# Attention probabilities copied by transfer into a one-pass-type tile before they are turned, with turns, values and ends two steps later

## The chip, the cores and the metric

The kernel runs on one core of a Trainium2 chip. The core has a matrix engine (TensorE, PE in the profile; its weight loads are PEld), a vector engine (DVE), a scalar engine (ACT), a general engine (GpSimd, POOL) and a queue engine (SyncE, SP), which works only as an issuer of transfers here. Transfers move between the chip's memory (SBUF) and the device memory, or within SBUF, on sixteen DMA engines. The metric is device time in microseconds (us) from start to end of one launch, the median of three runs.

## The reference

Two token batches, 512 and 256 tokens of width 1024, go through the same two layers with shared weights. Each layer adds half a SwiGLU feed-forward, then a token mixer, then half a SwiGLU again, each behind an RMS norm. The mixer of layer 0 is a gated linear recurrence, that of layer 1 is windowed attention, the part that the change touches:

```python
q = rope_partial(q.reshape(B, T, Hq, d))        # 16 query heads of 64
k = rope_partial(k.reshape(B, T, Hk, d))        # 4 key heads, each for 4 query heads
s = einsum('bnqhgd,bnkhd->bnhgqk', qb, kband) * d ** -0.5     # a block of 128 queries, 3 blocks of keys
s = where(abs(kpos - qpos) <= 128, s, -inf)
m = maximum(max(s), sink)
p = exp(s - m)
denom = sum(p) + exp(sink - m)
o = einsum('bnhgqk,bnkhd->bnqhgd', p / denom, vband)
return o.reshape(B, T, Hq * d) @ w_o
```

All values are 32-bit floats.

## The kernel before, in words

**Types.** A product of full precision is made of three products of the one-pass type F32R, a 32-bit type: an operand is split into a high part (ACT, L319) and the rest (DVE, L320), and `mm3` (L314 to L316) multiplies high by high, high by rest and rest by high.

**Tiles.** The score, key, value and output tiles of the attention come from one pool, `big`, with 21 slots (SLOTS) of 6 KB a partition; a tile takes a slot from its first writing until its last reading. There are eight PSUM banks (`ps`) and eight temporary tiles `tA`.

**The attention pipeline.** `swa` makes 24 `Unit`s: for each of 4 key heads, the 4 blocks of 128 queries of the first batch and the 2 of the second. A unit holds 4 query heads. Its query block sees 2 blocks of keys at an end of its sequence and 3 in the middle (`nkb`), so 16 units have 2 and 8 have 3. `pipeline` gives each part of each unit a step and a rank and runs all parts in this order; unit i starts at step t = 4i:

- `query` splits the queries, `turn` transposes them on PE in the type F32R (L1365, through the helper at L1181);
- `scores` takes a `big` tile `sc`, makes the products of one head (L1376, L1377), and DVE adds the band, scales and finds the minimum of the negated scores (L1379);
- `exps` on ACT (L1392), `sink` and `denominator` (L1398 to L1405), and at the end of `denominator` POOL multiplies the four heads' probabilities in place by the inverse sum (L1408), one instruction a head;
- `probs(j)`, at step t + 7 + j, transposes the four heads' probabilities of key block j by four PE instructions with the 32-bit type (L1414) into one PSUM bank and splits the bank into a high and a rest tile;
- `values(j)`, at step t + 9 + j, multiplies both with the values (L1426, L1427), adding up over the key blocks in one bank;
- `finish`, at step t + 8 + nkb, copies the sums out (L1435) and puts the halves of heads in place: for units 0 to 20 (`moved`) by two transfers on SP (L1439) and two adding transfers on POOL (L1440, issued at L147), for the last three by ACT and DVE (L1442, L1445).

Between these parts stand `extra` pieces: pieces of the query projection (`proj_tok`, matmuls at L314 to L316) up to step 66, the splits of finished outputs (`split_out`) from step 50, and 24 pieces of the first half of the output projection (`out_proj`) from step 66 to step 100.5. Behind the pipeline come the last splits and the second half of the output projection.

**What sets the order.** The program text gives priorities. The library that builds the program places each engine's instructions ahead of time by a model of their durations and of when their operands are ready: a later instruction whose operands are ready can be put ahead of an earlier one that still waits. On the chip every engine then works through its own fixed list, and an instruction that waits holds those behind it. SP's list holds the weight loads (L160, L194), which wait until a raw weight tile has been read (RAWBUFS is 4), and the transfers of `finish`. POOL's list holds the multiplies L1408, the adding transfers of `finish`, which wait for SP's transfers to land, and weight sums by transfer.

Of the kernel before, what the change touches and what calls it, by code (L numbers as in the profile page):

```python
# [9 lines left out]
F32 = mybir.dt.float32  # L10
F32R = mybir.dt.float32r
# [5 lines left out]
P = 128  # L17
# [11 lines left out]
GQ = 4  # L29
# [23 lines left out]
class Trunk:  # L53
# [1259 lines left out]
    def pipeline(self, units, extra):  # L1313
        events = []

        def at(step, rank, *calls):
            events.append((step, rank, len(events), calls))

        for i, u in enumerate(units):
            t = 4 * i  # L1320
            u.moved = i < 21
            at(t - (3 if i else 5), 5, u.query)
            at(t - 2, 3.5, u.turn)
            for h in range(GQ):
                at(t + h // 2, 0, lambda u=u, h=h: u.scores(h))
            at(t + 2, 2, u.sink)
            for h in range(GQ):
                at(t + 1 + h // 2, 2, lambda u=u, h=h: u.exps(h))
            at(t + 2, 2, u.denominator)
            for j in range(u.nkb):  # L1330
                at(t + 7 + j, 1, lambda u=u, j=j: u.probs(j))
                at(t + 9 + j, 4, lambda u=u, j=j: u.values(j))
            at(t + 8 + u.nkb, 4, u.finish)
        for step, call in extra:
            at(step, 3, call)
        for _, _, _, calls in sorted(events, key=lambda e: e[:3]):
            for c in calls:
                c()


class Unit:
# [59 lines left out]
    def denominator(self):  # L1401
        nc = self.k.nc
        den, sk = self.den, self.sk
        nc.vector.tensor_add(den, den, sk)
        nc.vector.reciprocal(den, den)  # L1405
        for i in range(GQ):
            p = self.sc[:, i, : self.nk]
            nc.gpsimd.tensor_scalar(p, p, den[:, i : i + 1], 1.0, ALU.mult, ALU.mult)  # L1408

    def probs(self, j):  # L1410
        k = self.k
        pt = k.ps()
        for i in range(GQ):
            k.nc.tensor.transpose(pt[:, i * P : (i + 1) * P], self.sc[:, i, j * P : (j + 1) * P], k.ident)  # L1414
        hi, lo = k.tmp(512, F32R), k.tmp(512, F32R)
        k.split(pt, hi, lo)
        self.split[j] = (hi, lo)
# [142 lines left out]
```

## Time and profile before

| | |
|---|---|
| median of 3 runs | 2769.42 us (2768.85 to 2770.11) |
| span of the profiled execution, first to last instruction | 2767.2 us |
| busy: PE, DVE, ACT, POOL | 99%, 80%, 50%, 16% of the span |
| attention pipeline (2063 to 2240 us): PE busy | 174.83 of 177.00 us |
| turns of probabilities (L1414) | 224 instructions, 270/272/300 ns least, median, most |

For the profiled execution the span alone is given, no time of its own beside it; the 2.2 us between its span and the median of the runs stand for what lies before the first and behind the last instruction.

How to read it: a row of the timeline has the start, the length, the engine, the line, the operation, the tiles written and read, and how many instructions it merges; a wait stands in brackets with what ended it. Matmuls are pipelined, so the length of one (0.39 us for 512 columns) is longer than the spacing between two starts (0.23 us). A row of groups has the busy time, the mean length of one, and the idle time before it. Lines with a q behind the engine belong to its sequencer, which issues transfers and waits.

### The profile page before, as it was taken

To read this page: it belongs to the slowest core of one execution; us is meant where nothing else is said; L and a number is where in the kernel's file an instruction comes from. 1 tells how busy PE (TensorE), PEld (TensorE's weight loads), DVE (VectorE), ACT (ScalarE), POOL (GpSimd) and SP (SyncE) were. 2 spreads that over 40 slices of the span, in tenths; PEclk is the share of its full clock that TensorE was granted. 3 is DMA by queue.
4 is the path that set the end of the run, shared out by engine and by line. 5 is a ranking of instruction groups with operands and counts; after the bars stand their busy time and mean duration, and the time that the engine had idled before them with its cause. 6 is when DMAs were issued, how large, how long until landed. Compare 5 with 4: busy or idle time off the path is not lost.

```text
span 2767.2 us, 40933 instructions
## 1 busy us (share of the span) xinstructions
PE 2745.0 (99%) x15117; PEld 2554.8 (92%) x15117; DVE 2206.5 (80%) x3766; ACT 1386.0 (50%) x2589; POOL 453.0 (16%) x491
## 2 busy tenths in 40 slices
PE   8999999999999999999999999999999999999998
PEld 8999999989999889999999999999888889999998
DVE  8788788767887888788878887887847868788877
ACT  7344444634455675444445543444458855444443
POOL 2111121200000101211111121111105611211111
PEclk9999999999999999999999999999999999999999
DMA  6554554851122743655444355544424422655443
GB/s 172 130 125 114 126 140 124 227 161 39 39 62 66 205 119 78 143 134 131 115 117 121 78 145 134 126 119 118 130 73 111 89 69 73 145 134 130 114 118 107
DMA packets 352040, 325.22 MB, mean 118 GB/s; under 512 B 14216, under 2 KB 271200, under 8 KB 351840
## 3 DMA queue, kind: packets, MB, share of 16 engines
q1 hardware_dynamic: 303040, 224.56, 27.7%
q0 software_dynamic: 44496, 84.56, 17.4%
q10 hardware_dynamic: 4304, 13.49, 1.3%
q8 instruction: 118, 1.93, 0.3%
q14 instruction: 82, 0.67, 0.1%
HBM read 225.82 MB, written 15.73 MB: 87 GB/s over the span
## 4 chain that ended last, share of the span: by engine, by line
PE 96%; DVE 2%; ACT 1%; DMA 1%; issue 0%; DVEq 0%; POOL 0%; SPq 0%; ACTq 0%; POOLq 0%
PE ps L513 42%; PE ps L577 21%; PE ps L315 6%; PE ps L316 6%; PE ps L314 6%; PE ps L760 5%; PE ps L823 3%; PE ps L928 1%; PE ps L1414 1%; PE ps L904 1%; PE ps L385 1%; PE ps L1426 0%; PE ps L1376 0%; PE ps L1427 0%; PE ps L1377 0%; PE ps L1181 0%
## 5 line engine op out<-in xcount | busy, mean ns | idle before, releaser
L513 PE MATMUL ps<-big,w 128*128 128x384 f32 x6720 | 1169.3, 334 | 0.0
L513 PEld LDWEIGHTS ps<-big,w 128*128 128x128 f32 x6720 | 1165.9, 188 | 1.7 <-ACT tA L530 0.2
L208 ACT CAST w<-wr 128x512 fp32r<-128x512 f32 x600 | 415.8, 707 | 689.2 <-PE ps L513 274.9
L577 PE MATMUL ps<-w,big 128*128 128x512 f32 x2520 | 575.7, 390 | 0.0
L577 PEld LDWEIGHTS ps<-w,big 128*128 128x128 f32 x2520 | 472.7, 188 | 98.0 <-ACT big L319 0.4
L209 DVE TENSOR_TENSOR w<-wr,w 128x512 fp32r<-128x512 f32 (+1 forms) x520 | 438.0, 846 | 145.9 <-ACT w L208 123.9
L147 POOL DMA_DIRECT2D s<-wr x126 | 109.8, 878 | 1250.3 <-DMA s<-in_ffn_w_dram 432.0
L599 DVE SCALAR_TENSOR_TENSOR x<-ps,x 128x512 f32<-128x512 f32 x468 | 302.4, 686 | 10.1 <-PE ps L316 10.0
L314 PE MATMUL ps<-big,w 128*128 128x384 f32 x640 | 219.6, 345 | 1.2 <-ACT w L175 0.9
L315 PE MATMUL ps<-big,w 128*128 128x384 f32 x640 | 215.7, 337 | 0.7 <-DVE big L320 0.7
L316 PE MATMUL ps<-big,w 128*128 128x384 f32 x640 | 214.6, 335 | 0.0
L319 ACT CAST big<-tA 128x384 fp32r<-128x384 f32 x296 | 148.0, 513 | 115.4 <-DVE tA L545 37.0
L147 POOL DMA_DIRECT2D wr<-wr x109 | 94.9, 871 | 518.3 <-DMA wr<-in_ffn_w_dram 165.9
L760 PE MATMUL ps<-w,big 128*128 128x512 f32 x756 | 177.1, 392 | 0.1
L320 DVE TENSOR_TENSOR big<-tA,big 128x384 fp32r<-128x384 f32 x296 | 168.0, 578 | 6.7 <-ACT big L319 4.7
L209 POOL TENSOR_TENSOR w<-wr,w 128x512 fp32r<-128x512 f32 x80 | 137.4, 1718 | 197.8 <-ACT w L208 195.8
L760 PEld LDWEIGHTS ps<-w,big 128*128 128x128 f32 x756 | 140.6, 188 | 29.1 <-DVE w L320 0.6
L215 DVE TENSOR_TENSOR wr<-wr,wr 128x512 f32<-128x512 f32 (+1 forms) x120 | 123.3, 1027 | 25.9 <-issue 23.6
L314 PE MATMUL ps<-w,big 128*128 128x512 f32 x336 | 134.6, 401 | 0.1
L316 PE MATMUL ps<-w,big 128*128 128x512 f32 x336 | 131.8, 392 | 0.5 <-DVE big L400 0.5
L315 PE MATMUL ps<-w,big 128*128 128x512 f32 x336 | 131.8, 392 | 0.0
L315 PEld LDWEIGHTS ps<-big,w 128*128 128x128 f32 x640 | 120.6, 188 | 2.0 <-DVE big L320 1.7
(214 smaller groups left out, 3504.0 us busy)
## 6 DMA issues: line engine op xcount, KB each, us to landing
wr<-in_ffn_w_dram SPq DMA_DIRECT2D x264, 512.0 KB, 4.0
s<-wr POOLq DMA_DIRECT2D x126, 256.0 KB, 4.8
s<-in_ffn_w_dram SPq DMA_DIRECT2D x120, 256.0 KB, 3.2
wr<-wr POOLq DMA_DIRECT2D x80, 256.0 KB, 3.8
wr<-in_hg_w_in_dram SPq DMA_DIRECT2D x32, 512.0 KB, 3.9
wr<-wr POOLq DMA_DIRECT2D x29, 512.0 KB, 4.6
spill<-x ACTq DMA_DIRECT2D x12, 512.0 KB, 4.0
kept<-big POOLq DMA_DIRECT2D x8, 768.0 KB, 9.7
```

The costliest lines, as they stand in the source:

```text
L147: self.nc.gpsimd.dma_start(out, src, accum_op=ALU.add)
L208: nc.scalar.copy(h, src)
L209: (eng or nc.vector).tensor_sub(l, src, h.bitcast(F32))
L314: nc.tensor.matmul(out, a[0], b[0], start=first, stop=False)
L315: nc.tensor.matmul(out, a[0], b[1], start=False, stop=False)
L316: nc.tensor.matmul(out, a[1], b[0], start=False, stop=last)
L319: self.nc.scalar.copy(hi, src)
L320: self.nc.vector.tensor_sub(lo, src, hi.bitcast(F32))
L513: self.nc.tensor.matmul(ps, a[x], b[y], start=first and k == 0 and i == 0, stop=k == 3 and i == 2, skip_group_check=True,)
L577: nc.tensor.matmul(ps, a[x], w[y], start=name == chain and kp == 0 and q == 0, stop=kp == 1 and q == 2, skip_group_check=True,)
L599: self.nc.vector.scalar_tensor_tensor(x, ps, c, x, ALU.mult, ALU.add)
L760: nc.tensor.matmul(ps, x[:, sl], y, start=fresh and k == 0 and q == 0, stop=k == 3 and q == 2, skip_group_check=True,)
```

## The change

Turns, values and end of every unit stand two steps later in the pipeline's order. In `denominator`, after each second multiply, a transfer on SP's queue copies two heads' probabilities from the score tile into a new `big` tile `pr` of the type F32R (as plain 32-bit data, so nothing is converted): two transfers a unit. `probs` then reads `pr` and turns it by the helper `transpose_r` (L1181), which writes the PSUM bank as F32R with the F32R identity. The number of turns, of splits and of value products is the same.

```diff
             for j in range(u.nkb):
-                at(t + 7 + j, 1, lambda u=u, j=j: u.probs(j))
-                at(t + 9 + j, 4, lambda u=u, j=j: u.values(j))
-            at(t + 8 + u.nkb, 4, u.finish)
+                at(t + 9 + j, 1, lambda u=u, j=j: u.probs(j))
+                at(t + 11 + j, 4, lambda u=u, j=j: u.values(j))
+            at(t + 10 + u.nkb, 4, u.finish)
...
             nc.gpsimd.tensor_scalar(p, p, den[:, i : i + 1], 1.0, ALU.mult, ALU.mult)
+            if i % 2:
+                if i == 1:
+                    self.pr = self.k.big([P, GQ, 3 * P], F32R)
+                two = slice(i - 1, i + 1)
+                nc.sync.dma_start(self.pr[:, two, : self.nk].bitcast(F32), self.sc[:, two, : self.nk])
...
         for i in range(GQ):
-            k.nc.tensor.transpose(pt[:, i * P : (i + 1) * P], self.sc[:, i, j * P : (j + 1) * P], k.ident)
+            k.transpose_r(pt[:, i * P : (i + 1) * P], self.pr[:, i, j * P : (j + 1) * P])
```

## The prediction

> **What bounds the kernel now.** I read the page first, then the busy time by stretches, then TensorE's groups and waits in the attention pipeline, then single rows of its timeline, and last the queues of POOL and SP. The page's first and fourth parts say that TensorE (PE) is the bound, over the whole span and on the chain that ended last:
>
> ```profile
> PE 2745.0 (99%) x15117; PEld 2554.8 (92%) x15117; DVE 2206.5 (80%) x3766; ACT 1386.0 (50%) x2589; POOL 453.0 (16%) x491
> PE 96%; DVE 2%; ACT 1%; DMA 1%; issue 0%; DVEq 0%; POOL 0%; SPq 0%; ACTq 0%; POOLq 0%
> ```
>
> The change touches only the attention pipeline, from the first scores to about 2240 us. The next rows are its stretch (columns: window, length, busy us of PE, weight loads, DVE, ACT, POOL, then clock, DMA share, GB/s), the group of the turns that the change retypes, and the first and last score product:
>
> ```profile
> 2063.00:2240.00 177.00, 174.83 (x1003) 149.32 (x1002) 136.42 (x427) 140.10 (x380) 93.73 (x138) 1.00 0.40 86
> L1414 PE MATMUL ps<-ident_r,big 128*128 128x128 f32 x224 | 33.7, 273 | 0.4 <-ACT tA L319 0.4
> L1376 PE MATMUL ps<-big,tA x96: 274/286/424, 2064.2 to 2222.4; 128*128 128x256 f32 x64, 128*128 128x384 f32 x32
> ```
>
> PE is busy 174.8 of 177.0 us here, so only 2.2 us of idle time can be won back, and PE time that is saved shortens the kernel as long as no new wait eats it. The 224 turns are 56 calls of four. 93 steps lie between the first and the last score product (unit 23's last is at step 93): (2222.4 - 2064.2) / 93 = 1.70 us a step, so two steps are 3.4 us.
>
> **Part 1: the retyped turns (the gain).** How long four turns hold PE is read from starts: from the first turn to the start of the second matmul behind it, less the normal spacing of the first one. The rows are of PE's timeline (start, length, line, ... count): eight old turns, then four of the one-pass type, which the query side (L1181) has already:
>
> ```profile
> 2226.36 1.03 PE L1414 MATMUL ps<-ident_r,big 128*128 128x128 f32 x8
> 2227.15 0.48 PE L314 MATMUL ps<-w,big 128*128 128x512 f32 x1
> 2227.46 0.40 PE L315 MATMUL ps<-w,big 128*128 128x512 f32 x1
> 2227.69 0.39 PE L316 MATMUL ps<-w,big 128*128 128x512 f32 x1
> ...
> 2121.36 0.46 PE L1181 MATMUL ps<-ident_r,s 128*128 128x128 f32 x4
> 2121.65 0.47 PE L1426 MATMUL ps<-tA,big 128*128 128x512 f32 x1
> 2121.96 0.39 PE L1427 MATMUL ps<-tA,big 128*128 128x512 f32 x1
> 2122.19 0.60 PE L1414 MATMUL ps<-ident_r,big 128*128 128x128 f32 x4
> 2122.54 0.48 PE L314 MATMUL ps<-w,big 128*128 128x512 f32 x1
> 2122.86 0.40 PE L315 MATMUL ps<-w,big 128*128 128x512 f32 x1
> ```
>
> A 512-wide matmul spaces 2227.69 - 2227.46 = 0.23. Eight old turns: 2227.46 - 2226.36 - 0.23 = 0.87, so 0.435 for four; the lone four at 2122.19: 2122.86 - 2122.19 - 0.23 = 0.44. Four one-pass turns: 2121.96 - 2121.36 - 0.23 = 0.37. The difference is 0.065 to 0.07 from these rounded times; with the two-digit rounding its bounds are 0.05 and 0.09. I take 0.07: 56 x 0.07 = **-3.9 us**, bounds -2.8 and -5.0.
>
> A row also weighs on how large this can be at all: four old turns cost 0.44 us, 56 x 0.44 = 25 us for all of them, and one-pass turns still cost 0.37. The Trainium skill (FP8 and Floating Point Precision, "TensorE Precision Notes") says that true FP32 takes four passes through the array; if an old turn were four passes and the new one a single pass, three quarters would go, 18 us rather than 3.9. The rows here do not agree: 224 turns leave 224 records, and a turn of the one-pass type is only a sixth cheaper.
>
> **Part 2: the copies (the cost).** Each of 24 units gets two copies on SP's queue, 48 in all. A unit with two key blocks copies 2 x 256 KB (16 units), one with three 2 x 384 KB (8 units): 14.7 MB. These rows bound them (DMA issues: KB each and median us to landing; then a queue's packets, MB and share; then SP and POOL rows):
>
> ```profile
> big<-tA SPq DMA_DIRECT2D x42, 64.0 KB, 2.2
> s<-in_ffn_w_dram SPq DMA_DIRECT2D x120, 256.0 KB, 3.2
> wr<-in_ffn_w_dram SPq DMA_DIRECT2D x264, 512.0 KB, 4.0
> big<-kept SPq DMA_DIRECT2D x8, 768.0 KB, 8.6
> q1 hardware_dynamic: 303040, 224.56, 27.7%
> 2220.83 1.25 SPq L1439 DMA_DIRECT2D big<-tA  x2
> ```
>
> Issuing costs SP 0.6 us a copy (1.25 for two), 30 us in all on a queue that mostly waits. On the DMA engines 14.7 / 224.56 of the share of q1 is 14.7 / 224.56 x 27.7% x 2767 = 50 us of all sixteen, so the stretch's share rises from 0.40 to about 0.68: not full. The trace shows no copy of this kind within the chip's memory at this size, so its landing is bounded: 2.2 us (64 KB, the only plain copy between tiles) below and 8.6 (768 KB) above. I take 3.2 for 256 KB and 4.0 for 384 KB, by the rows nearest in size. POOL's four multiplies are unchanged; the copy of heads 0 and 1 goes after the second, so only the last copy's issue and landing stand behind POOL: 0.6 + 3.2 = 3.8 us, or 4.6.
>
> What covers it is the move of two steps (3.4 us) plus the room there is now between POOL's last multiply and the unit's first turn. The tightest unit (4), a tight one with three blocks (20) and the last (23), POOL first and then PE:
>
> ```profile
> 2100.43 2.59 POOL L1408 TENSOR_SCALAR big<-big,stat 128x256 f32<-128x256 f32 x4
> 2103.56 0.38 PE L1414 MATMUL ps<-ident_r,big 128*128 128x128 f32 x2
> ...
> 2205.54 3.67 POOL L1408 TENSOR_SCALAR big<-big,stat 128x384 f32<-128x384 f32 x4 [3.25 <-PE ps L1377]
> 2210.67 0.60 PE L1414 MATMUL ps<-ident_r,big 128*128 128x128 f32 x4
> ...
> 2225.93 1.83 POOL L1408 TENSOR_SCALAR big<-big,stat 128x256 f32<-128x256 f32 x4 [0.42 <-DVE stat L1405]
> 2231.90 0.60 PE L1414 MATMUL ps<-ident_r,big 128*128 128x128 f32 x4
> ```
>
> The room is 0.5, 1.5 and 4.1 us. With 3.4 more it is 3.9, 4.9 and 7.5, against 3.8, 4.6 and 3.8: covered, by 0.1 to 3.7. At the upper landing (8.6) units 4 and 20 would miss by some 5 and 4 us. What then queues behind the waiting turn on PE is all that PE has next, the following units' scores and the projection's pieces, and DVE's reductions wait for those. Each unit's turns now wait for two transfers instead of POOL's one count; such an extra wait of PE's loader has a row:
>
> ```profile
> L1414 PEldq EVENT_SEMAPHORE  x16: 51/51/51, 2070.9 to 2218.6; - x16
> ```
>
> 48 of them would be 48 x 0.051 = 2.4 us, mostly hidden, since the loader is busy 149 of 177 us and runs ahead. For small misses and these I put **+0.5 us**; bounds 0 and +10. Without the two steps the tight units would miss by 3 us each, so the delay is the copy's cover and no gain of its own.
>
> **Part 3: the later turns, values and ends.** No work is added, only order. At the front two calls' turns and values come later, and the query projection's pieces (L314 to L316) fill in; at the end the last unit's turns, values and sum come 3.4 us later and the output projection has to cover. It can: its pieces for the first four blocks don't read the last two units, and at 12 matmuls x 0.23 = 2.8 us a block there are 11 us of them in one half of the columns, more than 3.4. An end moves its two transfers on SP and two adding transfers on POOL (L147) along; they now queue behind copies of later units on SP, which wait for POOL, while POOL's adding transfers wait for SP's. That ring costs at most an issue each, 1.25 us, while POOL is busy 94 of 177 us. I take 0, bounds -2.2 (all idle time of today goes) and +4.
>
> The old score tile is free once copied, but the copy lives till the last turn: a unit holds tiles for about 13 steps rather than 9 or 10, so one more of the 21 slots. By the code some 18 to 20 are taken around steps 50 to 60 (8 of the layer input, 2 keys, 2 values, 1 band, 2 held queries, 2 sums, 1 to 3 outputs, with 2 units' scores on top). A short wait for a slot is possible there; 0, up to +5.
>
> **The sum.** -3.9 + 0.5 = -3.4 on a span of 2767.2: 2763.8. The median of the runs shown is 2769.4, 2.2 over that span; I keep the 2.2: **2766.0 us**. A measurement of this kernel can tell about 0.2% from no change, 5.5 us: 2763.9 to 2775.0 counts as the same.
>
> **The rivals.**
>
> *Old waits vanish too.* The idle 2.2 us and the slow restarts round it come when ACT is late:
>
> ```profile
> PE ps L1376 <- ACT tA L1367: 1.3, 2, 1.1
> 2168.47 0.62 PE L1414 MATMUL ps<-ident_r,big 128*128 128x128 f32 x4
> 2170.20 0.38 PE L1376 MATMUL ps<-big,tA 128*128 128x256 f32 x1 [1.10 <-ACT tA L1367]
> ```
>
> With two steps' more turns and values in reserve PE would have work there: -3.9 - 2.2 = -6.1, or 2763.3. Against it: ACT's own load at that place does not change, and list orders move such gaps rather than close them.
>
> *SP's queue becomes the wait (the slower side).* SP's rows start one after the other, and its weight loads wait until DVE has read a raw tile (waits row: us in total, times, longest):
>
> ```profile
> 2086.31 7.42 SPq L160 DMA_DIRECT2D wr<-in_sw_w_o_dram  x4
> ...
> 2197.39 1.24 SPq L1439 DMA_DIRECT2D big<-tA  x2
> 2203.95 0.37 SPq L160 DMA_DIRECT2D wr<-in_ffn_w_dram  x1
> ...
> 2236.03 2.70 SPq L160 DMA_DIRECT2D wr<-in_ffn_w_dram  x2
> SPq L160 <- DVE w L176: 22.0, 6, 13.9
> ```
>
> SP stands from 2198.6 to 2203.95 and from 2222.1 to 2236.03 before such a load. Were the copies of units 19 and 23 ordered behind these, unit 23's would land at 2236.4 + 0.6 + 3.2 = 2240.2, though its turns want it at 2231.9 + 3.4 = 2235.3: 4.9 us. Behind the load at 2203.95 a copy loses up to 5.3 and behind the four from 2086.31 up to 7.4, each less its spare room, by estimate 2 and 3 left: +10 in all, -3.9 + 10 = +6.1, 2775.5. It decides once SP is held longer than the spare room above, 0.1 to 3.7 us. For it: six such waits, 13.9 us the longest. Against: the program's order puts transfers that are ready ahead of a load that is not (2220.83 before 2236.03).
>
> *A slot is short.* Around 2150 a unit's scores wait for a slot, the query pieces are used up early, and PE stands later. The estimate is bounded by one unit's period, 4 x 1.70 = 6.8 us; I price 6: -3.9 + 6 = +2.1, 2771.5.
>
> *The turns don't get cheaper*, since both kinds load weights at the same pace: 0 + 0.5, 2769.9. The 0.37 of L1181 speaks against it.
>
> *Four passes become one*: if a new turn held PE a quarter as long as an old one, 56 x 0.75 x 0.44 = 18 us would go, 2751; the 0.37 all but rules it out. (It is the Trainium skill's rule named in part 1.)
>
> **How the numbers follow.** Forecast 0.42 (own range 2763 to 2768.5; its lowest 0.06 count as faster), old waits vanish 0.17 (0.15 faster), SP's queue 0.20 (0.16 slower), slot 0.13 (0.03 slower), no cheaper turns 0.05, four passes 0.03 (faster). Faster: 0.06 + 0.15 + 0.03 = 0.24; slower: 0.16 + 0.03 = 0.19; same 0.57. The range runs from 2761 (old waits with the upper bound of the turns, -5.0 - 2.2 - 1) to 2778 (SP's queue with a little over); left out are the four passes and the outer parts of the two rivals, 0.17.
>
> **What would show it.** Turns at L1414's place at 0.37 a call, 224 records; a wait of PE for a transfer into the new tile under 1 us; SP's copies issued within 1 us of POOL's multiply; idle PE in the stretch still near 2 us; and the matmuls behind the pipeline at their old pace. PE rows with a release by that transfer of several us, or a copy that starts right behind a load's long wait, would prove the forecast wrong upwards; an idle time near nothing, downwards.

## The result, and the profile after

The changed kernel takes 2787.33 us (median of four launches) against 2769.25 for the kernel before, measured beside it: a ratio of 1.0063 [1.0050, 1.0077], 18 us slower. The forecast was 2766.0 with 2761 to 2778 around it. The profiled execution spans 2785.3 us against 2767.2, the same 18. One of the four launches ran at a granted clock of 0.849 and took 3023.11 us; it is left out of the ratio and of every reading below.

The page's busy time and its chain of the work that ended last:

```profile
PE 2748.7 (99%) x15117; PEld 2552.8 (92%) x15117; DVE 2211.8 (79%) x3766; ACT 1385.0 (50%) x2589; POOL 449.0 (16%) x491
PE 92%; ACT 2%; DVE 2%; DMA 1%; POOL 1%; issue 1%; DVEq 0%; SPq 0%; ACTq 0%; POOLq 0%
```

The engines do the same work; on the chain PE holds 92% instead of 96, and ACT, POOL and waits without an owner take what it lost. Ahead of the attention pipeline PE's busy time agrees with the kernel before within 1 us in each of five stretches up to 2063 us, and behind the pipeline the matmuls keep their old pace. The pipeline's stretch, by the busy time of each engine (columns as in the prediction), is where the time went:

```profile
2063.00:2240.00 177.00, 163.11 (x923) 135.85 (x923) 131.04 (x406) 129.04 (x361) 87.57 (x132) 0.96 0.59 160
2120.00:2140.00 20.00, 14.47 (x78) 11.93 (x77) 10.67 (x32) 10.54 (x33) 8.10 (x13) 0.89 0.58 158
2180.00:2200.00 20.00, 17.58 (x91) 14.20 (x92) 17.46 (x53) 15.14 (x44) 9.40 (x16) 0.83 0.57 155
```

PE idles 13.9 of 177 us, where it was 2.2, and the stretch holds 923 matmuls instead of 1003. The granted clock, 1.00 for this stretch before, falls to 0.89 and 0.83 in the stretches with the stalls. The DMA engines' share rose from 0.40 to 0.59; the forecast had 0.68.

The waits of the same stretch, to 2260 us (us in total, times, longest), of the changed kernel:

```profile
PE ps L1181 <- DMA big<-big: 6.3, 6, 2.7
SPq L1413 <- POOL big L1408: 113.5, 43, 21.8
SPq L1444 <- ACT tA L319: 7.7, 7, 3.6
```

and of the kernel before:

```profile
SPq L1439 <- ACT tA L319: 94.4, 14, 34.5
```

SP used to stand at the ends' transfers (L1439), waiting for what ACT makes. Now it stands at the copies (L1413), waiting for POOL, 113.5 us in 43 waits, and the ends' transfers (now L1444) stand behind them. How that goes round is in single rows of the changed kernel's timeline, SP and ACT first, then POOL, then PE. The end here is that of unit 5, the copies are those of unit 7:

```profile
2116.66 0.60 ACT L1440 COPY tA<-ps 128x512 f32<-128x512 f32 x1
2122.95 1.59 SPq L1413 DMA_DIRECT2D big<-big  x2
2124.63 1.36 SPq L1444 DMA_DIRECT2D big<-tA  x2
...
2111.61 2.87 POOL L1408 TENSOR_SCALAR big<-big,stat 128x256 f32<-128x256 f32 x4
2121.43 2.58 POOL L1408 TENSOR_SCALAR big<-big,stat 128x384 f32<-128x384 f32 x4
2129.82 1.99 POOL L147 DMA_DIRECT2D big<-tA  x2 [5.81 <-DMA big<-tA]
2131.08 3.01 POOL L1408 TENSOR_SCALAR big<-big,stat 128x384 f32<-128x384 f32 x4
...
2126.01 0.34 PE L1181 MATMUL ps<-ident_r,big 128*128 128x128 f32 x2 [1.13 <-DMA big<-big]
2129.01 1.00 PE L1181 MATMUL ps<-ident_r,big 128*128 128x128 f32 x6 [2.66 <-DMA big<-big]
2130.36 0.63 PE L315 MATMUL ps<-w,big 128*128 128x512 f32 x1
2130.79 0.63 PE L316 MATMUL ps<-w,big 128*128 128x512 f32 x1
2132.45 0.39 PE L314 MATMUL ps<-w,big 128*128 128x512 f32 x1
2132.68 0.39 PE L1432 MATMUL ps<-tA,big 128*128 128x512 f32 x1
```

ACT had the sums of unit 5 ready at 2117.26, but SP issues their transfers at 2124.63, 7.4 us later, because the copies ahead wait for POOL's multiplies from 2121.43 on. Those transfers land, POOL's adding transfers start at 2129.82 after 5.81 us of waiting, and only behind them in POOL's list come the next unit's multiplies, at 2131.08, for which SP's next copies wait. On the way the ends' landing is slow: the two transfers issued at 2124.63, beside the copies, landed after 4.3 us (median), where 2.2 is the median of the kernel before. The multiplies follow each other at 2131.08 - 2121.43 = 9.65 and 2121.43 - 2111.61 = 9.82 us. A unit of two and of three key blocks alike has four steps, 4 x 1.70 = 6.8 us, so POOL loses some 3 us a unit for as long as the ring runs, until the reserve (probabilities multiplied and copied ahead of their turns) is used up and PE waits for copies: 1.13 and 2.66 us here. After the pause PE's matmuls start 2130.79 - 2130.36 = 0.43 us apart instead of 0.23 (2132.68 - 2132.45) for about 3 us more. The Trainium skill (TensorE: Matmul & The Clock Gate, "Part 1: The HAM clock gate") says that PE falls to half its clock after an idle window of about 3.4 us and returns after about as long a busy one; the trace agrees about the half and the time back. The two pauses here add up to 3.79 us, with two turns between them, so neither of them alone is as long as that window.

### The profile page after: what moved, and what is told of

Same layout as the page of the kernel before. It is cut to its first block, busy times and chain, and to the rows that moved or that the text cites. A ratio compares the mean times of both kernels' runs of the same rounds, so it can differ in the third digit from the quotient of the medians.

```text
span 2785.3 us, 41086 instructions
## 1 busy us (share of the span) xinstructions
PE 2748.7 (99%) x15117; PEld 2552.8 (92%) x15117; DVE 2211.8 (79%) x3766; ACT 1385.0 (50%) x2589; POOL 449.0 (16%) x491
## 4 chain that ended last, share of the span: by engine, by line
PE 92%; ACT 2%; DVE 2%; DMA 1%; POOL 1%; issue 1%; DVEq 0%; SPq 0%; ACTq 0%; POOLq 0%
PE ps L513 42%; PE ps L577 21%; PE ps L315 6%; PE ps L314 6%; PE ps L316 6%; PE ps L760 5%; PE ps L823 3%; PE ps L928 1%; DMA big<-tA 1%; PE ps L1181 1%; PE ps L904 1%; PE ps L385 1%; POOL big L1408 0%; ACT big L1392 0%; ACT w L175 0%
## 5 line engine op out<-in xcount | busy, mean ns | idle before, releaser
L147 POOL DMA_DIRECT2D s<-wr x126 | 110.4, 883 | 1252.5 <-DMA s<-in_ffn_w_dram 438.1
L319 ACT CAST big<-tA 128x384 fp32r<-128x384 f32 x296 | 148.0, 513 | 114.1 <-DVE tA L545 36.2
L147 POOL DMA_DIRECT2D wr<-wr x109 | 95.5, 876 | 516.4 <-DVE w L209 196.2
```

The costliest lines, as they stand in the source:

```text
L147: self.nc.gpsimd.dma_start(out, src, accum_op=ALU.add)
L319: self.nc.scalar.copy(hi, src)
```

## The experiments

All differences below are against the kernel before as it was measured beside each (2768.4 to 2769.3 us). The list of every engine is planned anew for each kernel, so each run also has small shifts that are not its edit's. The runs stand here by question, not in the order in which they were made, so an expectation may name the time of a run that stands further down.

The expectations set four theories against each other. *Ring*: SP's copies wait for POOL and hold the ends' transfers, for which POOL waits. *Landing*: the copies' own way takes too long for the turns. *Delay*: the two later steps are the loss. *Traffic*: the copies' bytes lengthen the ends' transfers, and others wait for these. An edit also moves the line numbers below it: the ends' transfers on SP are L1439, L1444, L1448 or L1453, the copies L1413, L1414 or L1422, POOL's adding transfers L147 or L148.

### The parts one by one

**The delay alone**: before, with the three steps changed as in the change, and nothing else.

> The kernel before with turns, values and ends two steps later, no copies, old turns. Ring theory (the copies wait for POOL's multiplies on SP's list and hold the ends' transfers behind them, POOL's adding transfers wait for those to land, and the next multiplies stand behind POOL's adding transfers): the delay alone does no harm, 2769 within 3 us, idle time of PE in the attention pipeline near the old 2.2 us. Rival 'delay' (two steps more of live tiles and the later end are the loss): 2780 or more. Rival 'landing' (the copies' own way through the loaded DMA engines is the loss): 2769.

Measured 2773.95 us, 1.0019 [1.0010, 1.0027]: +5.1. The waits of ACT, this run first and then the kernel before:

```profile
ACT big L319 <- DMA big<-tA: 6.0, 3, 3.3
```

```profile
ACT big L319 <- DMA big<-tA: 1.7, 1, 1.7
```

The splits of finished outputs (`split_out`, ACT at L319) kept their steps while the ends moved two steps towards them, so ACT now stands before ends that have not landed. The delay was priced at nothing; it is not, and the ring theory's 2769 within 3 us was missed by 2.

**The type alone**: before, with POOL writing its product into a new F32R tile, no copies and the old steps.

```diff
+        self.pr = self.k.big([P, GQ, 3 * P], F32R)
...
-            nc.gpsimd.tensor_scalar(p, p, den[:, i : i + 1], 1.0, ALU.mult, ALU.mult)
+            nc.gpsimd.tensor_scalar(self.pr[:, i, : self.nk], p, den[:, i : i + 1], 1.0, ALU.mult, ALU.mult)
...
```

The turns then read the new tile through `transpose_r`, as in the change. The writing rounds the probabilities to the one-pass type, so their rest parts are left out of the values; the instructions are the same in number.

> The kernel before at its old steps, without copies: POOL's multiply writes its product into a new tile of the one-pass type and the turns read that. POOL rounds the probabilities to that type, so their rest parts are left out of the result. This is the retyping alone: 56 calls of turns at 0.37 instead of 0.44 us, 2765 to 2766, if the gain of the turns is as worked out; 2769 if the retyped turns are no cheaper in place; above 2775 if one more live tile a unit is already too much for the 21 slots.

Measured 2769.19, 1.0000 [0.9991, 1.0009]: not the 2765 to 2766 of the turns' gain, and not above 2775, which would have shown that one more live tile is too much. The turns did get cheaper, by PE's rows of this kernel:

```profile
2229.44 0.45 PE L1181 MATMUL ps<-ident_r,big 128*128 128x128 f32 x4
2229.73 0.46 PE L314 MATMUL ps<-w,big 128*128 128x512 f32 x1
2230.03 0.40 PE L315 MATMUL ps<-w,big 128*128 128x512 f32 x1
```

and its stretch by busy time:

```profile
2063.00:2240.00 177.00, 173.20 (x1008) 146.15 (x1007) 137.66 (x430) 139.75 (x380) 93.86 (x138) 1.00 0.41 89
```

Four take 2230.03 - 2229.44 - 0.23 = 0.36, but PE is idle 3.8 us of the stretch (177.00 - 173.20) instead of 2.2, by waits in the planned order of this run. The profiled execution spans 2764.8, 2.4 less than that of before; the medians show nothing of it. PE time that is saved is not all won, even without copies.

**The bytes alone**: before, with 48 copies of the change's shapes out of the keys' tile into a tile that nobody reads.

```diff
+            if i % 2:
+                if i == 1:
+                    pr = self.k.big([P, GQ, 3 * P])
+                two = slice(i - 1, i + 1)
+                nc.sync.dma_start(pr[:, two, : self.nk], self.kT[:, :, : self.nk].bitcast(F32))
```

> The kernel before with its steps and its turns, and 48 copies of the same shapes from the keys' tile into a tile that nobody reads: the bytes and SP's issues alone, no wait on POOL, no delay. Traffic theory: 2774 to 2780, with the ends' SP transfers landing after 2.8 us or more (2.24 before, median). Ring theory: 2767 to 2771. Output unchanged, since nothing reads the copies.

Measured 2771.54, 1.0011 [1.0001, 1.0020]: +2.8, between what the two theories said.

**Delay and bytes**: both of these edits together.

> The kernel before with the two steps' delay and the 48 copies taken from the keys' tile, read by nobody: the order and the bytes of the change, with no transfer that waits for POOL and no turn that waits for a copy. The run with the change's own copies and old turns (2794.2) differs from this one only in that SP's copies wait for POOL. Ring theory: about the sum of delay (+5.1) and bytes (+2.8), 2775 to 2780, so that 14 us or more of the 2794.2 belong to SP's wait for POOL. If delay and bytes together make the loss without any wait of SP: 2786 to 2795.

Measured 2777.39, 1.0034 [1.0024, 1.0044]: +8.6, about the sum of 5.1 and 2.8, as the ring theory had it.

**Copies that nobody needs**: the changed kernel, but `probs` turns the score tile in the old type, as before.

```diff
-            k.transpose_r(pt[:, i * P : (i + 1) * P], self.pr[:, i, j * P : (j + 1) * P])
+            k.nc.tensor.transpose(pt[:, i * P : (i + 1) * P], self.sc[:, i, j * P : (j + 1) * P], k.ident)
```

> The changed kernel, but the turns read the score tile with the old type as before; the copies are made and nobody reads them. Ring theory: the queues are as in the changed kernel, POOL's multiplies still come every 10 us in the worst stretch; turns are spared only the copy's issue and landing of some 4 us and pay the old price (+4): 2778 to 2790. Rival 'landing': nobody waits for a copy, 2769 to 2772. Rival 'delay': 2780 or more, the same as the run with the delay alone.

Measured 2794.22, 1.0091 [1.0077, 1.0105], 4 us above the ring theory's range and far from *landing*. It differs from the run before it in the tile that the copies read, so that here SP's copies wait for POOL. Three views of each, a stretch by busy time, the group of the ends' adding transfers (busy, mean ns, idle before) and SP's waits, first with the copies that wait:

```profile
2110.00:2200.00 90.00, 78.11 (x399) 62.60 (x398) 58.60 (x184) 59.42 (x167) 44.65 (x66) 0.91 0.58 152
```

```profile
L147 POOL DMA_DIRECT2D big<-tA x42 | 41.7, 1132 | 66.5 <-DMA big<-tA 50.2 <-ACT tA L319 9.6 <-ACT big L319 3.5
```

```profile
SPq L1413 <- POOL big L1408: 126.1, 44, 21.8
```

then with the copies out of the keys' tile, where SP has no such wait:

```profile
2110.00:2200.00 90.00, 86.28 (x500) 72.66 (x499) 71.02 (x222) 71.58 (x205) 56.91 (x80) 1.00 0.69 176
```

```profile
L147 POOL DMA_DIRECT2D big<-tA x42 | 41.2, 1106 | 40.8 <-DMA big<-tA 12.1 <-ACT tA L319 7.9 <-ACT tA L1367 5.3
```

With the same bytes and the same steps, SP's wait for POOL, with the ends' transfers behind it, costs 2794.22 - 2777.39 = 16.8 us. POOL waits 50.2 us for ends' transfers instead of 12.1, PE does 399 matmuls in 90 us instead of 500, and the clock falls from 1.00 to 0.91. No turn waits for a copy here: the ring works through POOL's list alone. The Trainium skill (DMA: Bandwidth & Descriptors, "Anatomy of one DMA") says that a transfer's wait for a semaphore is done by the issuing sequencer, not by the DMA engines; the 126.1 us that SP stands, with ready transfers behind it, agree.

The way from before to after is then: delay +5.1, bytes +3.4 (2777.39 - 2773.95), SP's wait for POOL +16.8, and the new turns, which also wait for the copies, 2787.33 - 2794.22 = -6.9; in all 18.4, against the 18.1 measured. Of the -6.9 the turns' own time explains about 4; the rest was not settled.

### Longer delay

**Two steps more**: the changed kernel with turns, values and ends four steps later than before. If the copies' landing were the trouble, more time would hide it.

> The changed kernel with turns, values and ends four steps later than in the kernel before instead of two. Ring theory: the ring's 10 us a unit is a pace, which no later step can hide, 2785 to 2795. Rival 'landing': 3.4 us more cover the late copies, 2775 to 2780 with the longer end.

Measured 2811.26, 1.0155 [1.0140, 1.0170], 24 us worse than the change itself, and outside both ranges. No turn waits for a copy any more; PE's longest waits are for ACT's copies of the turned queries (L1367), and DVE's scores (L1379) wait for copies to land:

```profile
PE ps L1376 <- ACT tA L1367: 14.4, 3, 8.0
DVE big L1379 <- DMA big<-big: 12.3, 3, 8.0
```

So more time does hide the copies' landing from the turns, and the kernel is slower all the same: that they land too late for the turns is not the main cause. Part of the 24 us is another loss. By the code, a score instruction can wait for a copy only where its tile takes a slot that the copy still reads, and with two steps more every unit holds its tiles longer. At 2168.15 one such wait of 8.04 us ends; ACT's exponentials waited 9.67 us for the scores, and PE's wait of 7.96 us ends behind them.

### Cutting the ring

**No ends' transfers**: all ends by ACT and DVE (`u.moved = False`), in the kernel before and in the changed one.

> The kernel before with no unit's end moved by transfers: all ends go by ACT and DVE as the last three do. It is the partner of the next run, and costs DVE 21 x 0.85 us more: 2770 to 2785 by either theory.

> The changed kernel with all ends by ACT and DVE: copies stay on SP, but POOL has no adding transfers and SP no ends' transfers, so the ring does not exist. Ring theory: against its partner it is within +5 us (delay 5, turns -4, small misses) instead of the 18 us between the kernels before and after. Rival 'landing': 12 us or more over its partner.

Measured 2772.49, 1.0014 [1.0005, 1.0023], and 2775.58, 1.0025 [1.0016, 1.0035]. Without ends on the queues the whole change, copies, delay and all, costs 2775.58 - 2772.49 = 3.1 us instead of 18, within the 5 us that the ring theory gave. Nearly all of the loss goes through the ends' transfers. SP stands before the copies even longer here than in the changed kernel (113.5 us):

```profile
SPq L1413 <- POOL big L1408: 129.6, 47, 21.8
```

That SP stands costs little by itself; what stands behind it counts.

**Ends from ACT's queue**: `nc.scalar.dma_start(dst, r(low[:HD, :]))` in `finish`, in place of SP's.

> The changed kernel with one edit: the ends' two plain transfers go out on ACT's queue, right behind ACT's own copy out of PSUM, so that SP's list holds copies and weight loads only. Same copies, same bytes, same turns. Ring theory: the ends' transfers leave within 1 us of ACT's copy, POOL's multiplies come every 6.6 to 7 us again, and the time falls to 2764 to 2771 (the turns' gain of 4 less what 42 issues cost ACT). Rival 'landing': the copies move as many bytes, 2783 or more. Rival 'delay': 2783 or more.

Measured 2783.78, 1.0053 [1.0041, 1.0066]. The stall at 2120 is gone, by the busy time and PE's waits:

```profile
2120.00:2140.00 20.00, 19.99 (x123) 16.87 (x122) 15.03 (x53) 16.49 (x49) 12.57 (x18) 1.00 0.74 199
```

```profile
PE ps L1432 <- DVE tA L320: 4.8, 6, 1.6
PE ps L1376 <- ACT tA L1367: 4.5, 6, 1.5
```

but ACT now issues 42 transfers, and PE waits for what ACT and DVE make, 4.5 and 4.8 us, against 1.5 and 3.1 in the changed kernel. The ring is cut and most of its gain paid away; the ring theory's 2764 to 2771 was missed, and the time just reaches the 2783 of its rivals. What ACT's issues cost was not measured by itself.

**Adding transfers later**: POOL's adding transfers are kept back and issued behind the next unit's multiplies.

```diff
+        with self.k.tc.issue_after(last.ins):
+            while self.k.adds:
+                self.k.into(*self.k.adds.pop(0))
...
-                k.into(dst, r(low[HD:, :]))
+                k.adds.append((dst, r(low[HD:, :])))
```

> The changed kernel; POOL's two adding transfers of an end are put behind the next unit's four multiplies on POOL's list instead of ahead of them, so that no multiply stands behind a landing. Nothing else is moved; no engine gets more work. Ring theory: POOL waits some microseconds less for the ends' transfers, multiplies come every 6.8 us, PE waits for copies under 1 us in all, and the time is 2770 to 2776 (the delay's own 5 over the kernel before, less the turns' 4, plus small misses). Rival 'landing' (a copy's own 3 to 5 us through loaded DMA engines is the loss): 2782 or more.

Measured 2787.85, 1.0069 [1.0054, 1.0084]: as slow as the change and 12 us above the ring theory's range, with other rows, of the busy time, of the adding transfers' group, and of ACT's timeline:

```profile
2120.00:2140.00 20.00, 19.88 (x125) 17.08 (x125) 14.20 (x54) 15.56 (x48) 13.66 (x21) 1.00 0.81 216
```

```profile
L148 POOL DMA_DIRECT2D big<-tA x42 | 40.9, 1142 | 4.6 <-DMA big<-tA 4.0 <-issue 0.3
```

```profile
2174.59 0.40 ACT L320 CAST big<-big 128x256 fp32r<-128x256 f32 x1 [6.23 <-DMA big<-tA]
```

POOL waits 4.6 us in all before these transfers instead of 62.4, and PE runs through 2120 to 2140. But the outputs are finished a unit later, and ACT stands 6.23 us before a split of one (and 6.57 us once more near the end); right behind these two stand the copies and splits for which PE has its two longest waits of this run, 6.34 and 5.33 us.

**Copies behind the ends on SP**: a unit's copies are put on SP after the ends' transfers of the unit two before it; POOL's list stays.

```diff
+                while k.copies:
+                    k.copies.pop(0)()
```

(in `finish`, pinned behind its last transfer on SP; `denominator` only notes the copies, but for units 0, 1 and 23, which issue them at once.)

> The changed kernel, but the copies of a unit are put on SP behind the ends' transfers of the unit two before it, so that an end's transfer no longer stands behind a copy that waits for POOL; POOL's adding transfers stay in their place, unlike in the run that moved them. Ring theory: 2766 to 2774, ends' SP transfers within 1 us of ACT's copy, POOL's multiplies 6.5 us apart. Traffic theory: 2777 to 2785. If the copies now come too late for the turns, which would be a third thing, PE rows with a release by a transfer into the new tile add up to over 5 us.

Measured 2783.89, 1.0056 [1.0041, 1.0071]. The third thing of the expectation came, over its 5 us; the waits of PE and of SP:

```profile
PE ps L1182 <- DMA big<-big: 6.8, 9, 2.2
SPq L1453 <- ACT tA L320: 47.2, 9, 8.4
```

SP stands at the ends again, as before the change. PE's waits for copies stay, 6.8 us where the changed kernel has 6.3.

**Copies from POOL's own queue**: `nc.gpsimd.dma_start` for the copies.

> The changed kernel, but the 48 copies are issued from POOL's queue behind POOL's own multiplies, so that no SP instruction waits for POOL and the ring of SP and POOL has no SP half; the bytes are the same. POOL issues 48 more transfers of about 0.65 us, 31 us on an engine that was busy 94 of 177 us. If the ring is all that costs (ring theory): 2766 to 2773, POOL's multiplies some 6.5 us apart everywhere. If the copies' 14.7 MB lengthen the ends' 64 KB transfers, and the output's splits and the buffers of the ends wait for these (traffic theory): 2777 to 2785, with waits of ACT or DVE for the ends' transfers of 3 us and more.

Measured 2784.27, 1.0061 [1.0045, 1.0078], from 2781.47 to 2792.23, of which the profiled launch is the slowest. POOL, by its busy time in the stretch, has become the crowded list, 122.40 us instead of 87.57:

```profile
2063.00:2240.00 177.00, 163.37 (x904) 134.82 (x903) 126.20 (x396) 126.54 (x355) 122.40 (x174) 0.95 0.58 156
```

The ring theory's 2766 to 2773 and 2774 missed in both of these runs. The traffic theory's 2777 to 2785 holds in both by the time; its mechanism does not show in the first, where the ends' transfers on SP land after 2.1 us (median), and may in the second, where they take 3.1, against 2.2 in the kernel before and 2.8 in the changed one.

### The output's splits

If late splits were all that `adds_later` lost, moving the splits too should free it. They stand up to six steps later here, those of the second batch last:

```diff
-            extra.append(((50, 58, 83)[n // 4] + 2 * (n % 4), ...
+            extra.append(((50, 60, 85)[n // 4] + 2 * (n // 2 % 2) + (6 if n >= 4 else 4) * (n % 2), ...
```

**Both moves** on the changed kernel, **the splits alone** on it, **the splits with the delay alone**, and **both moves on the kernel before**:

> The changed kernel with two edits: POOL's adding transfers behind the next unit's multiplies (as in the run adds_later), and the splits of finished outputs of key heads 1 and 2 moved from steps 58 to 64 and 83 to 89 to steps 60 to 68 and 85 to 93, those of the second batch last, so that ACT does not stand before the adding transfers' landing. Two-cause theory (the ring on SP and POOL in the middle of the pipeline, and ACT standing at the splits after an end that comes later): both are gone, 2764 to 2770. If the copies' landing or the live tiles were the loss: 2780 or more.

> The changed kernel with the splits moved as above, and POOL's list as in the changed kernel. Two-cause theory: the ring stays, ACT's standing goes: 2778 to 2784. If the ring is no cause of its own: 2770 or less.

> The kernel before with turns, values and ends two steps later and the splits moved as above; no copies. Theory: the delay's loss of 5 was ACT standing 6 us at the splits: 2767 to 2771. If it is the later end of the pipeline instead: 2773 to 2775 as with the delay alone.

> The kernel before with the two edits of the run both, at the old steps and without copies: what these edits bring by themselves. By the theory nothing to gain but 1.7 us of ACT's standing: 2766 to 2770, so that a lower time of the run both would be the retyped turns'.

Measured 2783.73, 1.0056 [1.0041, 1.0071]; 2792.01, 1.0087 [1.0072, 1.0102]; 2771.43, 1.0012 [1.0003, 1.0022]; 2771.96, 1.0014 [1.0005, 1.0024]. The first two missed what the theory said, by 14 and 8 us; the first lies in the range named for the copies' landing or the live tiles, and why the second is slower than the change itself was not settled. The third comes 0.4 us above its range: the moved splits win back half of the delay's 5.1. The fourth comes 2 above: the moves cost some 3 us by themselves at the old steps. In the kernel with both moves one stall of PE is the largest, by rows of POOL, SP, DVE and PE:

```profile
2168.59 1.92 POOL L148 DMA_DIRECT2D big<-tA  x2
2169.23 1.12 SPq L161 DMA_DIRECT2D wr<-in_sw_w_o_dram  x2
2170.44 1.32 SPq L1448 DMA_DIRECT2D big<-tA  x2
2174.98 1.51 SPq L1414 DMA_DIRECT2D big<-big  x2
2178.90 0.69 DVE L321 TENSOR_TENSOR tA<-ps,tA 128x512 fp32r<-128x512 f32 x1 [5.08 <-DMA big<-tA]
2179.65 0.79 PE L1436 MATMUL ps<-tA,big 128*128 128x512 f32 x1 [4.67 <-DVE tA L321]
```

DVE writes a temporary tile there, of which there are eight, and it waits for ends' transfers that read such a tile: two issued on POOL from 2168.59 on, two on SP from 2170.44. The wait ends at 2178.90, 10.3 and 8.5 us after these two rows begin. By the rows of DMA issues the two on POOL landed after 6.1 and 9.5 us and the two on SP after 8.2 (median), where before the medians are 3.0 and 2.2. Beside them lie two weight loads of 512 KB at 2169.23 and copies.

**Both moves without copies, and with copies that nobody waits for**: turns of the old type, then the same with the 48 copies out of the keys' tile.

> The kernel with the adding transfers and the output's splits moved (2783.7), without the copies: turns read the score tile in the old type; the two steps' delay and both moves stay. If what remains of the loss there comes with the copies (their bytes): 2770 to 2775. If it comes with the order, that is the delay and the moves themselves: 2780 to 2784.

> The kernel with both moves and no copies (2777.2), plus the 48 copies from the keys' tile, read by nobody. If the bytes are what the uncut kernel (2783.7) still loses there: 2782 to 2787. If it is that turns and SP wait for POOL and for the copies: 2777 to 2780, the bytes' price of before.

Measured 2777.17, 1.0029 [1.0018, 1.0041], between the two ranges named for it, and 2784.30, 1.0054 [1.0039, 1.0069], in the range named for the bytes. The ends' transfers in the rows of DMA issues (KB each, median us to landing), without and then with those copies:

```profile
big<-tA SPq DMA_DIRECT2D x42, 64.0 KB, 2.5
big<-tA POOLq DMA_DIRECT2D x42, 64.0 KB, 3.0
```

```profile
big<-tA SPq DMA_DIRECT2D x42, 64.0 KB, 2.9
big<-tA POOLq DMA_DIRECT2D x42, 64.0 KB, 3.7
```

With the ring cut in this way the order (delay and moves) costs 8.4 and the bytes 7.1, and that is all of it: 2784.30 is as slow as the kernel with the copies that matter (2783.73). So there the waits for POOL and for the copies cost no more than the turns give back. The bytes cost 2.8 in the kernel before and 7.1 in this order; that the ends have less reserve here would explain it, but was not tested by itself.

## Why the prediction was wrong

**The step that failed** is in part 3: "That ring costs at most an issue each, 1.25 us, while POOL is busy 94 of 177 us. I take 0". The ring was named, in the right place and with the right queues, and the term was mis-sized: the runs put 16.8 us on it. Two things were missed. What goes round is not an issue but a whole trip: multiply, wait and issue of the copies, issue and landing of the ends (4.3 us alone), adding transfers, 9.7 us in the rows above, against the 6.8 us that a unit has. And POOL's busy share says nothing about a list whose time is waiting: POOL was busy 87.57 of 177 us and yet set the pace.

**The later steps** were priced at 0 with bounds -2.2 and +4; alone they cost 5.1, beyond the bound. The part asked whether PE has other work meanwhile (it has) and not who reads the ends: the splits kept their steps.

**The copies** were priced at +0.5 with bounds 0 and +10. Their landing was sized well: medians of 3.1 us for both sizes in the pipeline, where 3.2 and 4.0 were taken. But the price looked only at the turns that wait for them. The bytes alone cost 2.8 to 3.4.

**The turns** were right in size, as the changed kernel's rows show:

```profile
2089.54 0.45 PE L1181 MATMUL ps<-ident_r,big 128*128 128x128 f32 x4
2089.83 0.46 PE L1431 MATMUL ps<-tA,big 128*128 128x512 f32 x1
2090.13 0.39 PE L1432 MATMUL ps<-tA,big 128*128 128x512 f32 x1
```

2090.13 - 2089.54 - 0.23 = 0.36, where 0.37 was forecast. That all of it would shorten the kernel was too much: in the run with the type alone nothing came.

**The rivals.** *SP's queue becomes the wait* had the right queue and the wrong reason: the copies did not queue behind weight loads, which wait less than before (14.8 us at L160 for DVE's tile instead of 38.3); the ends queued behind the copies. *A slot is short*: DVE's scores wait 3.1 us once for a copy to land, which by the code is such a slot. It is not the main loss: without the ends' transfers the same tiles are held and 3.1 us are all that the change costs. With four steps of delay these waits grow to 12.3 us. *Old waits vanish*, *four passes* and *turns that don't get cheaper* fall by the rows above. Of the signs named beforehand, a wait of PE for the new tile under 1 us and idle PE near 2 us failed clearly, at 2.7 us longest and 13.9.

**The sum again**, as an estimate from what was measured: even without any ring, delay and bytes cost 8.6 against 4 of the turns at best, so the change would lose some 5 us. No run with the change in it was as fast as the kernel before.

## What to carry to other kernels

Where an added transfer makes one in-order queue wait for an engine, and that engine's own list waits for a later transfer of the same queue, add up the whole trip, landing included, and set it against the period of the loop; busy shares do not show it. How long the queue stands is no measure either: it stood longer in the run where the change cost only 3 us. A step that is moved later takes its time from whoever reads its result at a fixed place, so follow the result to its last reader and not only PE to its next work. And a ring that is cut by moving one of its parts can cost as much elsewhere: four ways of cutting this one left 15 to 20 us.

## What the runs showed of the hardware

A pause of PE is paid for twice: after 1.13 and 2.66 us of waiting, matmuls started 0.43 us apart instead of 0.23 for about 3 us, and whole stretches of 20 us were granted 0.83 to 0.89 of the clock. Transfers of 64 KB, which land in 2.2 to 3.0 us in the kernel before, took 6.1 to 9.5 once beside weight loads and copies, at a DMA share of 0.77 over those 20 us; a mean share below 1 does not mean that a small transfer is quick.
